# The last output of a decoder step: residual added by TensorE instead of GpSimd

## The chip, the cores and the metric

The kernel runs on one core of one Trainium2 chip. TensorE (PE) multiplies, VectorE (DVE) and ScalarE (ACT) work elementwise and read TensorE's result banks, GpSimd (POOL) works elementwise on on-chip memory alone, and SyncE (SP) issues transfers. The metric is the device time of one execution in microseconds (us); a median over several runs is given.

## The reference, cut to what matters

One inference step of a decoder layer over 520 tokens (512 of a prompt, 8 samples), width 1024. It has a SwiGLU feed-forward, a token mixer and a second SwiGLU, each between two normalizations and added to the residual:

```python
def rmsnorm(x, g):
    y = xf * lax.rsqrt(jnp.mean(xf * xf, axis=-1, keepdims=True) + EPS) * g
def swiglu(x, w_gate, w_up, w_down):
    return (jax.nn.silu(x @ w_gate) * (x @ w_up)) @ w_down
...
x = x + 0.5 * rmsnorm(swiglu(rmsnorm(x, ffn1_pre_g), ffn1_w_gate, ffn1_w_up, ffn1_w_down), ffn1_post_g)
x = x + rmsnorm(m, mix_post_g)          # m: the token mixer
x = x + 0.5 * rmsnorm(swiglu(rmsnorm(x, ffn2_pre_g), ffn2_w_gate, ffn2_w_up, ffn2_w_down), ffn2_post_g)
```

The change concerns the last line's outer part alone: the normalization of the second feed-forward's output, the addition to x, and the store of the layer's output.

## The kernel before, in words

Everything is kept transposed: the 1024 channels are 8 tiles of 128 partitions (`KD` = 8), the tokens lie along the free axis in two halves of 260 (`HC`, `HALVES`). Products are made to f32 accuracy from operands that are split into a high and a low part, three matmuls each (`passes`, L408 to L410).

The order of instructions on every engine is the order in which the Python code issues them. A product calls `tick` as it goes on, and at each tick the waiting tasks (generators that were given to `spawn`) run up to their next `yield n`, which asks for n ticks of pause. When no products are left, `finish` ticks until all tasks are done, so what stands behind the last product is issued task by task without a pause.

`down` makes the feed-forward's last product, y = W h, tile by tile; the last tile (d = 7) is made for half 0 and then for half 1 (`staged`). For each tile and half, `evac` squares the result bank on ScalarE, adds the square to `acc[hf]` on VectorE (`square_sum`, L516 and L517) and writes y = bank times gain on VectorE (L664). With the last tile of a half it spawns `post`. In `post`, `rstd` sums `acc` over the partitions with TensorE (`sums`, L471: three pieces of 87 tokens against a column of ones), VectorE makes the mean `ms` (L463), GpSimd the power -1/2 `rs` (L465), and TensorE spreads it to all partitions into the bank `rb` (`spread`, L477: three f32 products with the identity). `gnext` is None for the last output alone. Then ScalarE copies `rb` to `u` (L574), and for each of the 8 tiles t = y * rb is made (L580), x = x + t (L584) and stored by SP (L585). GpSimd makes t for the tiles 1 and 4 and the additions for 1, 4 and 6, since it cannot read `rb` it reads `u`; VectorE makes the rest. `x` holds its tiles in pairs (`x_tiles`, 128 x 2 x 260; `x_of` gives one of a pair). `self.ident` is the 128 x 128 identity in f32 (the tile `cst`). There are 8 result banks. `slot` gives on-chip tiles out of a ring.

Of the kernel before, what the change touches and what calls it, by code (L numbers as in the profile page):

```python
# [9 lines left out]
AF = mybir.ActivationFunctionType  # L10
ALU = mybir.AluOpType
# [4 lines left out]
P = 128  # L16
D = 1024
KD = D // P
# [11 lines left out]
HC = TOK // 2  # L30
HALVES = ((0, HC), (HC, HC))
PIECES, PW = 3, -(-HC // 3)
# [138 lines left out]
class Kernel:  # L171
# [371 lines left out]
    def inverse_rms(self, acc, r, plus):  # L543
# [17 lines left out]
            r[hf] = out[:, c0 : c0 + n]  # L561
        self.hold_sums = False

    def post(self, y, acc, hf, gnext, xs, r, plus, plus_next):

        nc = self.nc
        c0, n = HALVES[hf]
        cs = slice(c0, c0 + n)
        self.hold = self.hold_sums = gnext is not None
        yield 1 if gnext is None else 2  # L570
        r2 = yield from self.rstd(acc, 1.0 / D, 2 if gnext is None else 3, plus and plus[0:PW, hf * PIECES : (hf + 1) * PIECES])
        if gnext is None:
            r2s = self.work("u", n)
            nc.scalar.copy(r2s, r2)  # L574
            ts = []
            for i in range(KD + 1):
                if i < KD:
                    alone = i in (1, 4)
                    ts.append(self.slot("t", (P, n)))
                    (nc.gpsimd if alone else nc.vector).tensor_tensor(ts[i], y[i][:, cs], r2s if alone else r2, ALU.mult)  # L580
                if i:
                    k = i - 1
                    xk = self.x_of(k, hf)
                    (nc.gpsimd if k in (1, 4, 6) else nc.vector).tensor_tensor(xk, xk, ts[k], ALU.add)  # L584
                    nc.sync.dma_start(out=self.a["yT"][:, hf, k], in_=xk)  # L585
                yield 1
            return
        if not hf:
            self.rooted = False
            self.leads = 0  # L590
            self.spawn(self.pre_rms(xs, r, plus_next))
        lag = 2
        for k in range(KD + lag):
            if k < KD:
                t = self.work("t", n)
                nc.vector.tensor_tensor(t, y[k][:, cs], r2, ALU.mult)
                xk = self.x_of(k, hf)
                nc.gpsimd.tensor_tensor(xk, xk, t, ALU.add)
            if k >= lag:
                xs[hf].append(self.split_x(k - lag, hf, gnext))  # L600
            if not hf and k == 1:
                self.prefetch(True, 1)
            yield 1
        if not hf:
            self.prefetch(True, 2)
# [44 lines left out]
    def down(self, xin, pieces, gpost, gnext, held, plus=None, plus_next=None, x_from=None, seven=None):  # L650

        nc = self.nc
        y = []
        acc = [self.work(f"acc{hf}", HC) for hf in range(2)]
        xs, r = [[], []], [None, None]
        begun = set()

        def evac(d, hf, ps):
            while len(y) <= d:
                y.append(self.slot("y"))  # L660
            c0, n = HALVES[hf]
            self.square_sum(acc[hf], ps, hf, hf not in begun, nc.vector)
            begun.add(hf)
            nc.vector.tensor_scalar(y[d][:, c0 : c0 + n], ps, gpost[:, d : d + 1], None, ALU.mult)  # L664
            if d == KD - 1:
                self.spawn(self.post(y, acc[hf], hf, gnext, xs, r, plus, plus_next))

        def job():
            ws, k = [], 0
            for cnt in pieces:  # L670
                ws.append((self.next_unit(), range(k, k + cnt)))
                k += cnt
            return ws

        def load_x():
            self.x = self.x_tiles()
            for hf in range(2):
                for k in range(0, KD, 2):
                    nc.sync.dma_start(out=self.x[hf][k // 2], in_=x_from[:, hf, k : k + 2])

        for d in range(0 if seven is None else KD, KD - held):
            if d == 2 and x_from is not None:
                load_x()
            ps = self.product(job(), xin, "dn")
            for hf in range(2):
                evac(d, hf, ps[hf])
        if seven:

            rest, first8, D = seven
            xin = [rest[hf] + [None] * KD for hf in range(2)]  # L690
            xin = [Both(rest[hf], first8[hf]) for hf in range(2)]
            pieces = (7, 7, 8)
            ps = self.product(job(), xin, "dn")
            for hf in range(2):
                evac(0, hf, ps[hf])
            for d in range(1, KD - 1, 2):
                self.down_pair(rest, D, lambda z, hf, c: evac(d + z, hf, c), load_x if d == KD - 3 else None)
        self.staged([job] * held, sum(pieces), xin, "dn", lambda j, hf, ps: evac(KD - held + j, hf, ps), False)
        return xs, r
# [1194 lines left out]
```

## Time and profile before

| | |
|---|---|
| median of 3 runs | 1206.64 us (1204.07 to 1208.16) |
| the profiled execution | 1205.19 us |
| its span, first to last instruction | 1203.4 us |
| TensorE matmuls busy | 1173.8 us, 98% of the span |
| VectorE, ScalarE, GpSimd busy | 915.9, 601.7, 280.8 us |
| last down product's end | 1187.5 us |
| last elementwise instruction's end (VectorE) | 1197.1 us |
| mean granted TensorE clock | 0.991 |

Rows of a chain or timeline read: start in us, duration in us, engine, tile and line; in a timeline the bracket behind it says how long the engine had been idle and which instruction released it. Rows of groups read: line, engine, operation, output<-input, shapes, count, busy us, mean ns of one. L1878 is the program's end, where every engine waits for its own work (a DRAIN) and for the others (EVENT_SEMAPHORE); POOLq and the like are the engines' sequencers.

### The profile page before, as it was taken

The page shows a single profiled execution, that of the slowest core. Times are in us where ns is not written, and L with a number is a line of the kernel's source. Part 1 is how long each engine was busy: PE and PEld are TensorE (multiplying, and loading weights), DVE is VectorE, ACT ScalarE, POOL GpSimd, SP SyncE. Part 2 cuts the span into 40 slices and gives each one's busy share as a digit, 9 for nine tenths or more (in the row PEclk, how much of TensorE's full clock was granted, in tenths as well). Part 3 has the DMA queues.
Part 4 walks back from the last instruction along what each step waited for, and adds up shares of the span by engine and source line. Part 5 has one row for each costly group of instructions (what it writes and reads, how often), then busy time and mean ns, then how long its engine had stood idle before and what let it go on. Part 6 is the DMA issues. An engine that isn't in the chain of part 4 may idle for free. (4 is left out here: it accounts for less than half of the span.)

```text
span 1203.4 us, 25466 instructions
## 1 busy us (share of the span) xinstructions
PE 1173.8 (98%) x9805; PEld 1161.0 (96%) x9805; DVE 915.9 (76%) x1952; ACT 601.7 (50%) x1387; POOL 280.8 (23%) x502
## 2 busy tenths in 40 slices
PE   8999999999999999999999999999999999999995
PEld 8999999999999999999999999998999999999994
DVE  8988888777557788888677777757888888867554
ACT  6655666544335466313354774335565666553330
POOL 4211111000005148755541100504211111000003
PEclk8999999999999999999999999999999999999998
DMA  6787777133352433322466753242687777322352
GB/s 195 214 202 181 185 189 180 37 115 96 98 173 60 144 124 103 106 81 76 110 200 214 232 179 124 88 159 71 180 235 199 176 189 183 81 80 82 98 170 71
DMA packets 79754, 170.90 MB, mean 142 GB/s; under 512 B 17104, under 2 KB 20080, under 8 KB 79632
## 3 DMA queue, kind: packets, MB, share of 16 engines
q1 hardware_dynamic: 67344, 144.98, 37.9%
q0 software_dynamic: 12288, 24.29, 11.4%
q8 instruction: 77, 1.26, 0.4%
q14 instruction: 45, 0.37, 0.1%
HBM read 157.37 MB, written 11.86 MB: 141 GB/s over the span
## 5 line engine op out<-in xcount | busy, mean ns | idle before, releaser
L408 PE MATMUL p<-xhl,whi 128*128 128x260 f32 x784 | 230.9, 294 | 0.0
L409 PE MATMUL p<-xhl,whi 128*128 128x260 f32 x784 | 221.8, 283 | 1.4 <-DVE xhl L506 1.4
L410 PE MATMUL p<-xhl,wlo 128*128 128x260 f32 x784 | 221.2, 282 | 1.7 <-DVE wlo L351 1.7
L351 DVE TENSOR_TENSOR wlo<-raw,whi 128x1024 fp32r<-128x1024 f32 (+2 forms) x121 | 142.2, 1181 | 52.5 <-ACT whi L350 50.8
L408 PE MATMUL sv<-th,w 128*128 128x260 f32 x592 | 167.5, 283 | 0.5 <-ACT q L833 0.5
L409 PE MATMUL sv<-tl,w 128*128 128x260 f32 x592 | 167.5, 283 | 0.0
L410 PE MATMUL sv<-th,w 128*128 128x260 f32 x592 | 167.0, 282 | 0.0
L409 PEld LDWEIGHTS p<-xhl,whi 128*128 128x128 f32 x784 | 148.0, 189 | 2.0 <-DVE xhl L506 1.8
L410 PEld LDWEIGHTS p<-xhl,wlo 128*128 128x128 f32 x784 | 147.6, 188 | 2.2 <-DVE wlo L351 2.2
L408 PEld LDWEIGHTS p<-xhl,whi 128*128 128x128 f32 x784 | 147.8, 188 | 0.7
L350 ACT CAST whi<-raw 128x1024 fp32r<-128x1024 f32 (+2 forms) x121 | 116.3, 971 | 32.8 <-DMA raw<-dn_in 16.4
L307 POOL DMA_DIRECT2D s<-gu_in x74 | 65.1, 970 | 283.5 <-DMA s<-gu_in 169.1
L369 DVE TENSOR_TENSOR w<-s,w 128x512 fp32r<-128x512 f32 x148 | 101.5, 688 | 38.0 <-ACT w L368 36.7
L410 PE MATMUL dn<-hh,wlo 128*128 128x260 f32 x448 | 126.6, 283 | 1.2 <-DVE wlo L351 1.2
L408 PE MATMUL dn<-hh,whi 128*128 128x260 f32 x448 | 127.1, 284 | 0.0
L409 PE MATMUL dn<-hl,whi 128*128 128x260 f32 x448 | 126.6, 283 | 0.0
L410 PE MATMUL sv<-xhl,w 128*128 128x260 f32 x444 | 125.5, 283 | 0.0
L408 PE MATMUL sv<-xhl,w 128*128 128x260 f32 x444 | 125.4, 282 | 0.0
L409 PE MATMUL sv<-xhl,w 128*128 128x260 f32 x444 | 125.3, 282 | 0.0
L408 PEld LDWEIGHTS sv<-th,w 128*128 128x128 f32 x592 | 111.4, 188 | 0.8 <-ACT q L833 0.7
L410 PEld LDWEIGHTS sv<-th,w 128*128 128x128 f32 x592 | 111.7, 189 | 0.0
L409 PEld LDWEIGHTS sv<-tl,w 128*128 128x128 f32 x592 | 111.5, 188 | 0.0
(397 smaller groups left out, 3265.5 us busy)
## 6 DMA issues: line engine op xcount, KB each, us to landing
raw<-gu_in SPq DMA_DIRECT2D x50, 512.0 KB, 4.7
raw<-win_in SPq DMA_DIRECT2D x49, 512.0 KB, 3.6
s<-gu_in SPq DMA_DIRECT2D x74, 256.0 KB, 5.4
s<-gu_in POOLq DMA_DIRECT2D x74, 256.0 KB, 5.2
raw<-dn_in SPq DMA_DIRECT2D x32, 448.0 KB, 3.4
a<-gu_in SPq DMA_DIRECT2D x37, 256.0 KB, 5.7
x<-x SPq DMA_DIRECT2D x32, 260.0 KB, 5.2
raw<-dn_in SPq DMA_DIRECT2D x16, 512.0 KB, 3.7
```

The costliest lines, as they stand in the source:

```text
L307: self.nc.gpsimd.dma_start(out=out, in_=term, accum_op=ALU.add)
L350: self.nc.scalar.copy(hi[:, ks], t[:, ks])
L351: self.nc.vector.tensor_tensor(lo[:, ks], t[:, ks], hi[:, ks].bitcast(F32), ALU.subtract)
L369: nc.vector.tensor_tensor(w[:, 1], t[i], w[:, 0].bitcast(F32), ALU.subtract)
L408: mm(ps, hi[:, k, :], xh, start=first, stop=False, skip_group_check=more)
L409: mm(ps, hi[:, k, :], xl, start=False, stop=False, skip_group_check=more)
L410: mm(ps, lo[:, k, :], xh, start=False, stop=last, skip_group_check=more)
```

## The change

The last output gets a function of its own, `post_last`; `post` keeps the two others. Five things differ.

- y is written in pairs of tiles (`yp`, 128 x 2 x 260), apart for each half, and t is made for a pair at once (128 x 520), `rb` being read twice by a broadcast. The stores of half 0 and of half 1's last pair are for pairs.
- In half 1 the last tile's square isn't added to `acc`. TensorE sums `acc` (seven squares) and the last square `sq` apart; two `ms` follow one another on VectorE, the second taking the first as its addend.
- ScalarE's copy `u` is gone, and GpSimd's ten elementwise instructions. GpSimd makes the two powers.
- In half 1, tiles 0 to 5 are added by TensorE: the identity times x into a bank `xo` (three of these stand ahead of the spread, three behind it), then the identity times t onto it. ScalarE copies the bank into x, and SP stores each tile.
- In half 0, and for half 1's last pair, VectorE adds t to x in pairs.

```diff
+    def post_last(self, pairs, acc, sq, hf, plus):
...
+        yield 1
+        ps = self.bank("ss")
+        plus = plus[0:PW, hf * PIECES : (hf + 1) * PIECES]
+        self.sums(ps, acc, PIECES)
+        if sq is not None:
+            m = self.small("ms", [P, PIECES])
+            nc.vector.scalar_tensor_tensor(out=m[0:PW], in0=ps[0:PW, 0:PIECES], scalar=1.0 / D, in1=plus, op0=ALU.mult, op1=ALU.add)
+            plus = m[0:PW]
+            ps = self.bank("ss")
+            self.sums(ps, sq, PIECES)
+        _, r = self.root(ps, PIECES, 1.0 / D, plus)
+        banks = []
+
+        def begin(upto):
+            while len(banks) < upto:
+                banks.append(self.dbank("xo", HC))
+                mm(banks[-1], self.ident, self.x_of(len(banks) - 1, hf), start=True, stop=False, skip_group_check=True)
+
+        if hf:
+            begin(3)
+        else:
+            yield 2
+        rb = self.spread(r).unsqueeze(1).to_broadcast([P, 2, HC])
+        if hf:
+            begin(KD - 2)
+        for i in range(half):
+            x = self.x[hf][i]
+            t = self.slot("t", (P, 2, HC))
+            tt(t, pairs[hf][i], rb, ALU.mult)
+            if not hf:
+                yield 1
+            if hf and i < half - 1:
+                for z in range(2):
+                    k = 2 * i + z
+                    mm(banks[k], self.ident, t[:, z], start=False, stop=True, skip_group_check=True)
+                    nc.scalar.copy(x[:, z], banks[k])
+                    nc.sync.dma_start(out=out[:, hf, k], in_=x[:, z])
+                continue
+            tt(x, x, t, ALU.add)
+            nc.sync.dma_start(out=out[:, hf, 2 * i : 2 * i + 2], in_=x)
+            if not hf:
+                yield 1
...
@@ evac @@
+            else:
+                while len(pairs[hf]) <= d // 2:
+                    pairs[hf].append(self.slot("yp", (P, 2, HC)))
+                out = pairs[hf][d // 2][:, d % 2]
+            sq = None
+            if gnext is None and hf and d == KD - 1:
+                sq = self.work("s", n)
+                nc.scalar.activation(sq, ps, AF.Square)
+            else:
+                self.square_sum(acc[hf], ps, hf, hf not in begun, nc.vector)
             begun.add(hf)
-            nc.vector.tensor_scalar(y[d][:, c0 : c0 + n], ps, gpost[:, d : d + 1], None, ALU.mult)
-            if d == KD - 1:
+            nc.vector.tensor_scalar(out, ps, gpost[:, d : d + 1], None, ALU.mult)
+            if d == KD - 1 and gnext is None:
+                self.spawn(self.post_last(pairs, acc[hf], sq, hf, plus))
+            elif d == KD - 1:
                 self.spawn(self.post(y, acc[hf], hf, gnext, xs, r, plus, plus_next))
```

GpSimd's queue at the end of the program, as one piece of the difference. `rs` is the power; the rows below the first are those of half 0, the second power and half 1.

```order
 L465 TENSOR_TENSOR rs_16353<-ms_16351,mhalf 87x3
-L580 TENSOR_TENSOR t_16381<-y_15439,u_16371 128x260
-L584 TENSOR_TENSOR x_16168<-x_16168,t_16381 128x260
-L580 TENSOR_TENSOR t_16411<-y_15844,u_16371 128x260
-L584 TENSOR_TENSOR x_16170<-x_16170,t_16411 128x260
-L584 TENSOR_TENSOR x_16171<-x_16171,t_16431 128x260
-L465 TENSOR_TENSOR rs_16455<-ms_16453,mhalf 87x3
-L580 TENSOR_TENSOR t_16467<-y_15439,u_16463 128x260
-L584 TENSOR_TENSOR x_16172<-x_16172,t_16467 128x260
-L580 TENSOR_TENSOR t_16479<-y_15844,u_16463 128x260
-L584 TENSOR_TENSOR x_16174<-x_16174,t_16479 128x260
```

One more addition, for tile 7, follows before; now the second power is the queue's last work.

TensorE's queue before, from the last three of the down product's matmuls to the end:

```order
L408 MATMUL dn_2776_16334<-hp_2609_15109,whi_2771_16258 128x260
L409 MATMUL dn_2776_16334<-hp_2609_15109,whi_2771_16258 128x260
L410 MATMUL dn_2776_16334<-hp_2609_15109,wlo_2772_16259 128x260
L471 MATMUL ss_2791_16449<-ones_93,acc1_2579_14927 87x1 x3
L477 MATMUL rb_2794_16459<-cst_122,rs_2793_16455 128x87 x3
```

And now, behind the same three matmuls (`ss` are the sums, `xo` the banks of the addition, `cst` is the identity):

```order
L471 MATMUL ss_2786_16432<-ones_93,acc1_2579_14927 87x1 x3
L471 MATMUL ss_2788_16438<-ones_93,s_2785_16429 87x1 x3
L586 MATMUL xo_2791_16446<-x_2750_16172,cst_122 128x260
L586 MATMUL xo_2792_16448<-x_2750_16172,cst_122 128x260
L586 MATMUL xo_2793_16450<-x_2751_16173,cst_122 128x260
L477 MATMUL rb_2794_16452<-cst_122,rs_2790_16444 128x87 x3
L586 MATMUL xo_2795_16456<-x_2751_16173,cst_122 128x260
L586 MATMUL xo_2796_16458<-x_2752_16174,cst_122 128x260
L586 MATMUL xo_2797_16460<-x_2752_16174,cst_122 128x260
L604 MATMUL xo_2791_16446<-t_2798_16462,cst_122 128x260
L604 MATMUL xo_2792_16448<-t_2798_16462,cst_122 128x260
```

Four more of L604 follow. Three products moved ahead of the spread, and nine stand behind it where there was nothing.

VectorE's queue now, from the last tile's y to the end; before, sixteen instructions of 128x260 stood here (acc, y, one t and one x of half 0, `ms`, then eleven of half 1):

```order
L710 TENSOR_SCALAR yp_2766_16232<-dn_2776_16334,gh_124 128x260
L576 SCALAR_TENSOR_TENSOR ms_2787_16436<-ss_2786_16432,plus2_13_128 87x3
L463 SCALAR_TENSOR_TENSOR ms_2789_16442<-ss_2788_16438,ms_2787_16436 87x3
L598 TENSOR_TENSOR t_2798_16462<-yp_2617_15153,rb_2794_16452 128x520
L598 TENSOR_TENSOR t_2799_16470<-yp_2672_15518,rb_2794_16452 128x520
L598 TENSOR_TENSOR t_2800_16478<-yp_2715_15867,rb_2794_16452 128x520
L598 TENSOR_TENSOR t_2801_16486<-yp_2766_16232,rb_2794_16452 128x520
L608 TENSOR_TENSOR x_2753_16175<-x_2753_16175,t_2801_16486 128x520
```

The addition to `acc` is gone from here, the mean has become two instructions, and one of half 1's four pairs is still added here.

More of the change, by code (lines that the diff above doesn't have):

```diff
@@ L562, in inverse_rms @@
         self.hold_sums = False
+    def post_last(self, pairs, acc, sq, hf, plus):
+        nc = self.nc
+        tt, mm = nc.vector.tensor_tensor, nc.tensor.matmul
+        half = KD // 2
+        out = self.a["yT"]
+        yield 1
[38 more added lines that the diff above has]
+                yield 1
     def post(self, y, acc, hf, gnext, xs, r, plus, plus_next):
@@ L568, in post @@
         cs = slice(c0, c0 + n)
[L569 to L587, printed above, removed]
+        self.hold = self.hold_sums = True
+        yield 2
+        r2 = yield from self.rstd(acc, 1.0 / D, 3, plus and plus[0:PW, hf * PIECES : (hf + 1) * PIECES])
         if not hf:
@@ L656, in down @@
         begun = set()
+        pairs = [[], []]
         def evac(d, hf, ps):
-            while len(y) <= d:
-                y.append(self.slot("y"))
             c0, n = HALVES[hf]
-            self.square_sum(acc[hf], ps, hf, hf not in begun, nc.vector)
+            if gnext is not None:
+                while len(y) <= d:
+                    y.append(self.slot("y"))
+                out = y[d][:, c0 : c0 + n]
+            else:
[8 more added lines that the diff above has]
+                self.square_sum(acc[hf], ps, hf, hf not in begun, nc.vector)
             begun.add(hf)
-            nc.vector.tensor_scalar(y[d][:, c0 : c0 + n], ps, gpost[:, d : d + 1], None, ALU.mult)
-            if d == KD - 1:
+            nc.vector.tensor_scalar(out, ps, gpost[:, d : d + 1], None, ALU.mult)
+            if d == KD - 1 and gnext is None:
+                self.spawn(self.post_last(pairs, acc[hf], sq, hf, plus))
+            elif d == KD - 1:
                 self.spawn(self.post(y, acc[hf], hf, gnext, xs, r, plus, plus_next))
```

## Prediction

> **What bounds the kernel now.** I read the page's head first, then the chain of waits over the last 16 us, because the diff touches only the last output.
>
> ```profile
> span 1203.4 us, 25466 instructions
> PE 1173.8 (98%) x9805; PEld 1161.0 (96%) x9805; DVE 915.9 (76%) x1952; ACT 601.7 (50%) x1387; POOL 280.8 (23%) x502
> ```
>
> TensorE is busy for 98% of the span, and nothing of the change lies under its long run of products. What can move is the tail behind the last product. Its chain, rows of half 1:
>
> ```profile
> 1187.53 0.40 ACT s L516
> 1187.95 0.43 DVE acc L517
> 1188.38 0.40 DVE y L664
> 1188.78 0.33 DVE t L580
> 1189.11 0.15 DVE ms L463
> ...
> 1189.33 1.00 POOL rs L465
> ...
> 1190.38 0.92 PE rb L477 x6
> ...
> 1191.32 0.38 ACT u L574
> ...
> 1191.72 0.44 DVE t L580
> ...
> 1192.71 0.74 DVE t L580 x2
> ...
> 1196.61 0.51 DVE x L584
> ```
>
> The last square waits for nothing but the last product (1187.51). Then come the addition to the sum of squares, the mean `ms`, GpSimd's power `rs`, its spread over the partitions `rb`, ScalarE's copy `u`, and sixteen elementwise instructions until 1197.12. But the chain ends at 1197.12 and the span at 1203.4. What fills the 6.3 us between is in the instructions of the program's end, L1878 (first four rows: the whole trace, with shortest/median/longest duration in ns and first and last start; then the stretch 1198 to 1200; then 1202.5 to 1202.75):
>
> ```profile
> L1878 POOLq DRAIN  x3: 51/93/6696, 1195.9 to 1203.1; - x3
> L1878 PEldq DRAIN  x2: 13/475/937, 1190.4 to 1203.0; - x2
> L1878 ACTq DRAIN  x2: 14/210/406, 1191.3 to 1202.9; - x2
> L1878 DVEq DRAIN  x2: 19/283/547, 1196.6 to 1202.9; - x2
> ...
> L1878 SPq EVENT_SEMAPHORE  x8: 28/28/28, 1199.1 to 1199.5; - x8
> L1878 SPq DRAIN  x2: 7/7/7, 1199.6 to 1199.6; - x2
> ...
> L1878 POOLq EVENT_SEMAPHORE  x1: 17/17/17, 1202.7 to 1202.7; - x1
> ```
>
> The last store has landed at 1199.1, when SP's eight end waits begin, and SP is through at 1199.6. TensorE, ScalarE and VectorE ended their drains with their last work (1196.6 + 0.55 = 1197.15 for VectorE). GpSimd's drain began at 1195.9 and took 6.70 us: until 1202.6. The end follows 0.8 us later. So **the kernel ends with GpSimd's drain**, 3.0 us after SP was ready. GpSimd's last work, and the stores that SP issued in half 1:
>
> ```profile
> 1195.98 0.85 POOL L584 TENSOR_TENSOR x<-x,t 128x260 f32<-128x260 f32 x1 [1.04 <-DVE t L580]
> 1192.81 0.92 SPq L585 DMA_DIRECT2D yT_out<-x  x2
> 1196.86 0.81 SPq L585 DMA_DIRECT2D yT_out<-x  x2
> yT_out<-x SPq DMA_DIRECT2D x8, 130.0 KB, 1.8
> ```
>
> The drain outlasts the last GpSimd instruction (end 1196.83) by 5.8 us. Two issues in a row stand 0.47 us apart (0.81 - 0.34), so the last store was issued at 1197.33 and landed 1.77 us later.
>
> **The change part by part.** *1. Last square's sums apart.* Gone from the path are acc, y and a left-over t of half 0 between square and `ms`. The prices:
>
> ```profile
> 1188.44 0.62 PE L471 MATMUL ss<-ones,acc 128*87 128x1 f32 x6 [0.94 <-DVE acc L517]
> 1188.30 0.48 DVE L664 TENSOR_SCALAR y<-dn,gh 128x260 f32<-128x260 f32 x1
> 1182.44 0.38 ACT L574 COPY u<-rb 128x260 f32<-128x260 f32 x1 [3.57 <-PE rb L477]
> L537 DVE TENSOR_TENSOR sq<-sq,sq 128x520 f32<-128x520 f32 x14 | 9.8, 699 | 0.6
> ```
>
> The first three sums (of the seven older squares) run right behind the last product, under ScalarE's square, which ends at 1187.93. The second three start at 1187.99 and end at 1188.61 (0.62); the second mean runs from 1188.65 to 1188.80, the power from 1188.87 instead of 1189.33: **-0.46**. VectorE must be free: y starts when the square ends (1187.97, 0.48), the first mean follows by 1188.5. Ahead of them in its queue stand half 0's eight instructions of 128x520, at 0.70 us each with the 0.1 us overlap of independent neighbours: from 1182.44 (rb is done; it waits no more for ScalarE) to about 1187.85. That is 0.1 us of cover; were it missing, each tenth over it would be lost.
>
> *2. Power, spread, ScalarE's copy.* The power stays 1.00, to 1189.87. TensorE's three x products stand ahead of the spread now; it is free from 1188.57 to 1189.91. For their price there is no row of 128x260 in plain f32; the nearest:
>
> ```profile
> 500.03 0.39 PE L1353 MATMUL po<-st,rp 128*128 128x128 f32 x2
> 500.26 0.39 PE L1354 MATMUL po<-rv,sT 128*128 128x128 f32 x2
> L1545 PE MATMUL pV<-pack,AT 32*32 32x32 f32 x64 | 2.3, 194 | 0.0
> L1167 PE MATMUL tr<-cst,cv 128*128 128x128 f32 x48 | 7.4, 277 | 0.0
> L408 PE MATMUL p<-xhl,whi 128*128 128x260 f32 x784 | 230.9, 294 | 0.0
> ```
>
> One f32 product is two records. With 128 columns the pair takes 0.225 us, 0.11 a record. A record grows from 194 to 277 ns between 32 and 128 columns, 0.86 ns a column; 260 columns give 260 x 0.86 = 0.22 a record, **0.44 a product**. The bounds: 0.24, if a record costs the 0.12 us at which the 128x260 records of the long products follow each other (1173.8 us / 9805), and 0.88, if the clock is halved. I take 0.44, from the f32 rows. Three are 1.32, until 1189.89: just under the power, so the spread is not late. It ends at 1190.83. The copy `u` is gone, with its two gaps: t starts at 1190.87 instead of 1191.72. **-0.39** more.
>
> *3. The elementwise part.* VectorE: four t of 0.70 (0.6 apart), then one addition of 0.70; done at about 1194.1. TensorE: the spread's issue is over at 1190.67 (0.17 before its end), three x products to 1191.99, by then the first t (1191.57) is there; six t products to 1194.63, the result 0.17 later (277 ns of a record less its 0.11), ScalarE's copy 0.38 (each hides under the next product), so SP issues the sixth store at 1195.25 and the pair's store, waiting behind it, 0.47 later at 1195.72. TensorE's nine products set this, not VectorE. Before: 1197.33. The last issue is **-1.61** early, of which steps 1 and 2 made 0.85; 0.76 is new. With 0.24 a product, SP's seven issues of 0.47 become the bound and it is another 0.45.
>
> *4. The last store is twice as long* (260 KB for 130 KB):
>
> ```profile
> 1198.20:1198.40 0.20, 0.00 (x0) 0.00 (x0) 0.00 (x0) 0.00 (x0) 0.00 (x0) 0.50 0.84 302
> 1198.60:1198.80 0.20, 0.00 (x0) 0.00 (x0) 0.00 (x0) 0.00 (x0) 0.00 (x0) 0.50 0.08 21
> ```
>
> (stretches: us, busy of PE, PEld, DVE, ACT, POOL, then clock, DMA share, GB/s). 133 KB more at 302 GB/s: **+0.44**; the bounds are 0 (the other stores of half 1 are through, the path has room) and 0.9 (half the rate, behind a backlog). Landing: 1195.72 + 1.77 + 0.44 = 1197.93, SP ready at 1198.45.
>
> *5. GpSimd only makes the power.* Its five elementwise instructions of half 1 go to VectorE and TensorE (paid in 3). Its last work ends at 1189.87, and a drain of 5.8 us behind it ends at 1195.7, 2.8 us before SP. Then SP is last and the end stands 0.8 us behind it: 1199.25. Removed: **-3.0**, the time from SP's readiness to the drain's end. Bounds: 0, if the drain ends by something else than its own work, and 3.0, which is all there is.
>
> *6. At no cost:* the pair tiles for y (same number of tiles; the first writes into the last pair wait for old products, as y's did), four stores of half 0 in place of eight, and half 0's additions on VectorE, all under the last stage's products.
>
> Sum: -0.46 - 0.39 - 0.76 + 0.44 - 3.0 = **-4.2 us**. The profiled execution took 1205.19 (span 1203.4): 1201.0 after. The median shown is 1206.64, 1.45 above it, so I forecast **1202.4**.
>
> **The rivals.** *The drain stays.* If its 6.7 us hang on the end of the other engines or on the last store (it ended 3.5 us after that landed) and not on GpSimd's own last instruction, term 5 is nothing and 1.2 us are left: 1205.4. For it: no other long drain is in this trace to show what sets it. Against: it is a bare drain without a wait, begun next to the last GpSimd instruction, and three other engines' drains ended with their own work.
>
> *TensorE cold or f32 dearer, the slower side.* The clock after the spread of before:
>
> ```profile
> 1191.00:1192.00 1.00, 0.28 (x3) 0.12 (x2) 0.28 (x1) 0.38 (x1) 0.23 (x1) 1.00 0.00 0
> 1192.00:1193.00 1.00, 0.00 (x0) 0.00 (x0) 0.96 (x3) 0.00 (x0) 0.92 (x2) 0.84 0.00 0
> 1193.00:1194.00 1.00, 0.00 (x0) 0.00 (x0) 1.00 (x3) 0.00 (x0) 1.00 (x2) 0.50 0.34 115
> ```
>
> The granted clock falls to half at about 1192.7, 1.4 us after TensorE's last work. With P a product, the last issue is at 1188.57 + 12 P + 1.85 once 3 P outlasts the power; the gain of 3.0 less 0.44 is eaten at 1199.9, so from P = 0.79 the change loses. At 0.88 the issue is at 1200.98 and the time 1.1 us longer: 1207.7. Against it: the clock was still 1.00 after 1.3 us of waiting for the power, and after the change that gap is filled with products. The Trainium skill, "TensorE: Matmul & The Clock Gate", Part 1 (the HAM clock gate), says that a free-running window of about 3.4 us in which the array is idle halves the clock. By that rule nine products without a gap would stay at full clock and the sum would stand; a window that happens to close early, as the drop 1.4 us after the spread suggests, speaks for this rival.
>
> *The products at 0.24:* 0.45 better, 1202.0; it lies in the first case's range.
>
> **How the numbers follow.** The forecast (drain hidden, products between 0.24 and about 0.5) 0.80, drain stays 0.15, TensorE cold 0.05. The bound of about 0.3%, what a measurement of this kernel can tell from no change, is 3.6 us. The three runs lie from 1204.07 to 1208.16, so a median is uncertain by over 1 us. A gain of 4.2 is over 3.6 in two of three such measurements: 0.53 from the first case, 0.02 from the second, none from the third: faster 0.55; same 0.42; slower 0.03. Range: down to 1200.0 (all bounds on the good side, -5.1, and the median's scatter of 1.5), up to 1206.0 (the drain stays and 0.6 of scatter).
>
> **What would show it.** In the profile after: the power about 1.4 us behind the last product's end instead of 1.8; no ScalarE instruction between spread and first t; GpSimd's drain still 6 to 7 us long but begun near the power and over before SP's last end wait; records of `xo` 0.22 us apart at clock 1.00; the last store issued some 8.2 us after the last product (9.8 before). Wrong would be: a drain that ends later than SP again, a clock of 0.50 before the sixth store, or VectorE late for the mean because half 0 is not done at 1187.9.

## The result, and the profile after

| | before | after |
|---|---|---|
| median | 1206.17 us (9 runs, from 1204.07) | 1202.42 us (9 runs, 1200.28 to 1203.04) |
| profiled execution, its span | 1205.19, 1203.4 | 1200.41, 1198.6 |
| last down product's end | 1187.51 | 1187.05 |
| from there to the span's end ("the tail") | 15.89 | 11.55 |

The ratio of after to before is 0.9967, 95% interval 0.9958 to 0.9977; one run of before at 1908.33 us is left out of it. The forecast was 1202.4. Of the 4.8 us between the two spans 4.34 lie in the tail; 0.46 lie ahead of the last product, where the change leaves TensorE's products as they were; in the variants of the changed kernel below, that point lies anywhere between 1186.44 and 1190.54, so this is scatter. All comparisons of single profiles below are therefore made by the tail. A span is given to 0.1 us, and a tail from one profile is no finer than that.

The chain of waits of the changed kernel, behind the last product (start, duration, engine, tile, line):

```profile
1186.91 0.14 PE dn L410
...
1187.07 0.40 ACT s L706
...
1187.51 0.62 PE ss L471 x6
1188.14 1.42 PE xo L586 x6
1189.56 0.65 PE rb L477 x6
1190.21 1.35 PE xo L586 x6
1191.56 2.64 PE xo L604 x12
...
1194.23 0.38 ACT x L605
```

Where VectorE, GpSimd and ScalarE took turns before, TensorE works from 1187.51 to 1194.2 almost without a gap. A product of 128x260 in f32 costs 1.42 / 3 = 0.47, 1.35 / 3 = 0.45 and 2.64 / 6 = 0.44 us. The other engines' rows from the timeline, with what each waited for in brackets:

```profile
1188.41 0.85 POOL L465 TENSOR_TENSOR rs<-ms,mhalf 87x3 f32<-87x3 f32 x1 [7.50 <-DVE ms L463]
1190.25 2.52 DVE L598 TENSOR_TENSOR t<-yp,rb 128x520 f32<-128x520 f32 x4 [1.92 <-PE rb L477]
1192.04 2.57 ACT L605 COPY x<-xo 128x260 f32<-128x260 f32 x6 [4.58 <-PE xo L604]
1192.44 2.79 SPq L606 DMA_DIRECT2D yT_out<-x  x6
1195.32 0.40 SPq L609 DMA_DIRECT2D yT_out<-x  x1
```

The power starts 1188.41 - 1187.05 = 1.36 us behind the last product (1.82 before). The first t starts 3.20 behind it (4.21 before), but its first pair is ready at about 1190.94, and TensorE comes to it only at 1191.56. The last store is issued 8.27 behind the last product (9.82 before). Now the program's end, whose line is L1926 here: three rows of the whole trace, then one of the stretch 1197.2 to 1198.

```profile
L1926 SPq EVENT_SEMAPHORE  x11: 17/28/28, 1195.8 to 1198.5; - x11
L1926 POOLq DRAIN  x3: 51/102/6689, 1188.4 to 1198.3; - x3
L1926 SPq DRAIN  x3: 7/7/7, 1197.8 to 1198.1; - x3
...
L1926 SPq EVENT_SEMAPHORE  x6: 17/28/28, 1197.5 to 1198.0; - x6
```

GpSimd's drain is still there and as long as ever, 6.69 us, but it begins at 1188.4 with the power and is over at 1195.1. The last store has landed at 1197.5, SP is ready at 1197.8, and the end follows 0.8 later: SP, not GpSimd, is last by 2.7 us. The stores and the clock (stretch, busy of the five engines, granted clock, DMA share, GB/s):

```profile
1193.20:1196.90 3.70, 0.99 (x5) 0.53 (x3) 0.30 (x1) 1.22 (x4) 0.00 (x0) 1.00 0.81 284
1197.60:1198.60 1.00, 0.00 (x0) 0.00 (x0) 0.00 (x0) 0.00 (x0) 0.00 (x0) 1.00 0.00 0
```

The clock stayed at 1.00 to the end, and half 1's output moved in one stretch of 3.7 us at 284 GB/s; before, the same bytes trickled out over about 5 us.

### The profile page after: what moved, and what is told of

It reads as the page before. It is cut to its first block, busy times and chain, and to the rows that moved or that the text cites. A ratio compares the mean times of both kernels' runs of the same rounds, so it can differ in the third digit from the quotient of the medians.

```text
span 1198.6 us, 25498 instructions
## 1 busy us (share of the span) xinstructions
PE 1179.1 (98%) x9835; PEld 1165.9 (97%) x9835; DVE 913.7 (76%) x1943; ACT 603.1 (50%) x1391; POOL 273.5 (23%) x492
## 3 DMA queue, kind: packets, MB, share of 16 engines
q0 software_dynamic: 12288, 24.29, 11.1%
```

## The experiments

Four questions: what sets GpSimd's drain, whether it alone makes the gain, which of the other steps lie on the path, and what sets the end now.

**1. A late GpSimd instruction.** An addition of 128x520 whose result nobody reads is put on GpSimd behind the last VectorE addition.

```diff
+            if hf:
+                z = self.slot("z", (P, 2, HC))
+                nc.gpsimd.tensor_tensor(z, x, t, ALU.add)
```

> The changed kernel with one more GpSimd instruction (128x520, into a tile that nothing reads) behind half 1's last addition on VectorE, which ended at 1193.50 in the changed kernel's profile. If the end of the program waits for GpSimd's drain, the drain begins near 1193.5 and, at its 6.69 us of both profiles, ends near 1200.2 (or near 1200.8 if it is 5.83 us behind the end of an instruction of some 1.5 us); the tail from the last product to the end grows from 11.55 to 13.9 to 14.6 us and the time from 1202.4 to 1204.8 to 1205.4. Rival: the gain came from the shorter chain and the stores alone, the drain is no cause: the tail stays 11.55 and the time 1202.4.

Measured: 1202.97 us (10 runs), ratio to the kernel before 0.9983 (0.9973 to 0.9992). The timeline's row of the added instruction, the two drains, and the head of the page (last product's end 1186.54):

```profile
span 1201.0 us, 25500 instructions
1193.15 1.28 POOL L612 TENSOR_TENSOR z<-x,t 128x520 f32<-128x520 f32 x1 [4.41 <-DVE x L608]
L1929 POOLq DRAIN  x3: 51/102/7107, 1193.1 to 1200.7; - x3
L1929 SPq DRAIN  x3: 7/7/7, 1197.2 to 1200.5; - x3
```

SP is ready at 1197.2 and waits until the drain ends at 1200.2; the tail is 14.5, 2.9 longer than without the addition, as expected. The time missed the expectation: 1202.97 for 1204.8 to 1205.4. The kernel before was faster beside it (1205.24), but that makes up only 0.9 of it. By the ratios (0.9967 and 0.9983) the addition cost 0.16%, about 1.9 us, and with the width of the two intervals anything from 0 to 4 us fits, so the weight lies on the tail. The drain has become longer (7.11 us), and ends 5.8 us behind the addition's end (1194.43).

**2. The same with a tiny instruction**, a copy of 128x1 in the same place:

```diff
+            if hf:
+                z = self.small("z", [P, 1])
+                nc.gpsimd.tensor_copy(z, x[:, 0, 0:1])
```

> As the run before, but the added GpSimd instruction copies a 128x1 column. If the drain is 6.69 us from its own start, its end is the same as with the long instruction, near 1200.2 on the changed kernel's clock, tail 13.9 us; if it is 5.83 us behind the last instruction's end, it ends a good 1 us earlier than with the long one, tail about 13.2 us. Rival without the drain: tail 11.55 us.

Measured: one run, 1205.6 us, all of it later ahead of the tail (last product's end 1190.54), so only the tail is read: 13.26.

```profile
span 1203.8 us, 25499 instructions
1197.05 0.19 POOL L612 COPY z<-x 128x1 f32<-128x1 f32 x1 [4.31 <-DVE x L608]
L1929 POOLq DRAIN  x3: 51/102/6017, 1197.0 to 1203.6; - x3
```

This drain takes 6.02 us and again ends 5.8 us behind the instruction's end (1197.24). So the drain follows GpSimd's own last instruction by a fixed 5.8 us, whatever that instruction was; its row is longer only because it begins while the instruction still runs. The rival that it hangs on the stores or the other engines has fallen: in the changed kernel the drain was over at 1195.1, before the last store was issued (1195.32).

**3. The kernel before without GpSimd in half 1.** All else of the change is left out; VectorE makes all sixteen elementwise instructions of half 1.

```diff
-            alone = i in (1, 4)
+            alone = not hf and i in (1, 4)
...
-    (nc.gpsimd if k in (1, 4, 6) else nc.vector)
+    (nc.gpsimd if not hf and k in (1, 4, 6) else nc.vector)
```

> The kernel before with one part of the change alone: GpSimd's five elementwise instructions of half 1 go to VectorE, everything else as before (no product adds, no pairs, the ScalarE copy stays). Sixteen VectorE instructions of 128x260 at 0.34 us apart end at about 1197.2, as the mixed ones did (1197.12). By the drain theory the drain is over at about 1196 and the end stands 0.8 us behind SP's 1199.6: 1200.4, tail from 15.9 to 12.9 us, time 1203.2 for 1206.2 of before (ratio 0.9975). Rival: the drain is no cause, tail 15.9 or a little longer, ratio 1.000.

Measured: 1201.85 us (10 runs), ratio 0.9975 (0.9965 to 0.9984), the ratio that was expected.

```profile
1188.08 0.99 POOL L465 TENSOR_TENSOR rs<-ms,mhalf 87x3 f32<-87x3 f32 x1 [1.31 <-DVE ms L463]
L1878 POOLq DRAIN  x3: 51/93/6832, 1188.0 to 1198.9; - x3
L1878 SPq DRAIN  x3: 7/7/7, 1198.4 to 1198.7; - x3
```

Its last square starts at 1186.28, so the last product ended at about 1186.26 and the tail is 1199.2 - 1186.26 = 12.94: 2.95 less than before. About two thirds of the tail's gain (2.95 of 4.34) are had by two edited conditions. VectorE alone is done at 1195.96, 9.70 behind the last product; with GpSimd's help it was 9.61. VectorE's own additions took up to 0.97 us beside GpSimd's and 0.42 alone. So GpSimd's help saved 0.1 us of work and cost 3.0 at the end.

**4. The last square back into `acc`**, in the changed kernel:

```diff
-            if gnext is None and hf and d == KD - 1:
+            if False:
                 sq = self.work("s", n)
```

> The changed kernel with the last square added to acc again by VectorE and the sums made once, as in the kernel before; all else stays. The tail from the last product's end to the span's end is 11.55 us in the changed kernel. Theory (step 1 is worth its 0.46 us and all of it lies on the path): the power starts about 1.8 us behind the last product instead of 1.36, and the tail is 12.0 us. Rival (the x products and the stores set the end, the power's start has room): the tail stays within 0.15 of 11.55.

Measured (one run, 1203.31; its chain):

```profile
span 1201.5 us, 25483 instructions
1189.36 0.14 PE dn L410
...
1189.52 0.40 ACT s L516
1189.94 0.44 DVE acc L517
1190.43 0.62 PE ss L471 x6
1191.05 1.42 PE xo L586 x6
```

The tail is 1201.5 - 1189.50 = 12.0. Everything behind the sums has the changed kernel's durations, only later: step 1 is worth its 0.45 in full.

**5. ScalarE's copy `u` back between spread and t**, in both halves:

```diff
-        rb = self.spread(r).unsqueeze(1).to_broadcast([P, 2, HC])
+        rb = self.spread(r)
+        u = self.work("u", HC)
+        nc.scalar.copy(u, rb)
+        rb = rb.unsqueeze(1).to_broadcast([P, 2, HC])
```

> The changed kernel with ScalarE's copy u put back between the spread and the first t of each half: t waits for it, and begins about 0.4 us later. By the prediction's step 2 the copy costs its 0.39 us on the path: tail 11.9 us in place of 11.55. Rival, read from the changed kernel's trace (the first t is ready at 1190.94, TensorE is busy with the x products until 1191.56): TensorE's nine products set the end, a t that is ready at 1191.34 is still in time, and the tail stays 11.5 to 11.6.

Measured: one run, 1202.42, last product's end 1188.71, span 1200.6: tail 11.89, as the prediction's step 2 has it. But the profile shows another way to it. From the timeline:

```profile
1188.81 0.70 DVE L611 TENSOR_TENSOR x<-x,t 128x520 f32<-128x520 f32 x1
1190.32 0.84 POOL L465 TENSOR_TENSOR rs<-ms,mhalf 87x3 f32<-87x3 f32 x1 [7.74 <-DVE ms L463]
1192.15 0.38 ACT L594 COPY u<-rb 128x260 f32<-128x260 f32 x1 [3.03 <-PE rb L477]
1193.31 2.90 PE L607 MATMUL xo<-t,cst 128*128 128x260 f32 x12
```

The copy of half 0 made half 0's additions later: the last ends 0.80 behind the last product, in the changed kernel 0.38. That held up VectorE's y and the mean, and the power starts at 1.61 instead of 1.36. So 0.25 of the 0.34 came from half 0. This number alone would have confirmed a wrong reason.

**6. The copy in half 1 alone** tells the two apart:

```diff
+        if hf:
+            u = self.work("u", HC)
+            nc.scalar.copy(u, rb)
```

> The changed kernel with ScalarE's copy u put back in half 1 alone. With the copy in both halves the tail was 11.89 in place of 11.55, but there half 0's additions had also become 0.4 us later, and the power started 1.61 instead of 1.36 us behind the last product. Here half 0 is untouched, so the power starts at 1.36 again, the first t about 3.6 behind the last product (3.20 without the copy). Theory (the copy lies beside TensorE's x products, which end 4.51 behind the last product, when the first t is ready at about 4.3): tail 11.5 to 11.65. Rival (the copy is on the path with its 0.39): 11.9.

Measured: one run, 1200.4, span 1198.6; its chain:

```profile
1186.81 0.14 PE dn L410
...
1190.10 1.35 PE xo L586 x6
1191.46 2.75 PE xo L608 x12
```

The power is at 1.36 again, TensorE turns to the t products 4.51 behind the last product as without the copy, and they take 2.75 instead of 2.64. The tail is 1198.6 - 1186.95 = 11.65. The copy costs 0.10 here, not 0.39. That holds with TensorE's additions in place. Where VectorE makes them (experiment 3 with the copy, experiment 7 without), the first t starts 1.34 and 0.94 us behind the spread's start, so there the copy delays VectorE by 0.40.

**7. No additions on TensorE**: VectorE adds all four pairs of half 1 (`begin` and its products left out).

```diff
-            if hf and i < half - 1:
+            if False:
```

> The changed kernel without TensorE's additions: in half 1 VectorE adds all four pairs, and all four are stored as pairs. VectorE then has eight instructions of 128x520, 0.70 us each with 0.1 overlap of neighbours that do not wait for each other: from 3.1 us behind the last product (no x products ahead of t) to about 8.2 to 8.6, so the last store is issued at 8.2 to 8.6 where it was 8.27. Theory (VectorE on whole pairs is nearly as fast; the gain of step 3 comes from pairs and the missing GpSimd steps): tail 11.5 to 11.9. Rival (the 0.76 us of step 3 hang on TensorE's additions): tail 12.3.

Measured: one run, 1200.26, span 1198.5. From the timeline, the last addition, and SP's drains:

```profile
1189.63 0.70 DVE L594 TENSOR_TENSOR t<-yp,rb 128x520 f32<-128x520 f32 x1 [1.92 <-PE rb L477]
...
1194.39 0.70 DVE L604 TENSOR_TENSOR x<-x,t 128x520 f32<-128x520 f32 x1
...
L1922 SPq DRAIN  x3: 7/7/7, 1197.7 to 1198.0; - x3
```

The last square starts at 1186.46, the last product ended at 1186.44. VectorE is done 8.65 behind it, just past the upper end of what I expected, and the tail is 12.06, between the theory (11.5 to 11.9) and the rival (12.3). TensorE's twelve products, with ScalarE's copies, are worth about 0.5 us against three more additions on VectorE: something, but the smaller part of the gain.

**8. Four tiles on TensorE, two pairs on VectorE**, a better balance by the issue times:

```diff
-            begin(KD - 2)
+            begin(KD - 4)
...
-            if hf and i < half - 1:
+            if hf and i < half - 2:
```

> The changed kernel with four tiles added by TensorE and two pairs by VectorE in half 1. If the last store's issue sets the end (TensorE's nine products behind the spread and seven issues in a row), the last issue comes at 1194.3 in place of 1195.32 and the tail falls from 11.55 to 10.5 us, time 1201.4. Rival: the stores are bound by their transfer (1.07 MB at the 284 GB/s of the changed kernel): the last byte comes only as much earlier as the first store does, 0.5 us: tail 11.05. Second rival: nothing, since the end hangs elsewhere: 11.55.

Measured: 1201.61 us (5 runs), ratio 0.9968 (0.9955 to 0.998), the changed kernel has 0.9967. Last product's end 1187.01, span 1198.1, tail 11.1.

```profile
1193.99 0.88 SPq L609 DMA_DIRECT2D yT_out<-x  x2
L1926 SPq DRAIN  x3: 7/7/7, 1197.2 to 1197.5; - x3
```

The last issue came 0.8 us earlier (two in 0.88, the second at about 1194.47, so 7.46 behind the last product), the tail shrank by 0.45. That is the first rival's number (11.05) and not the theory's (10.5). Its reason does not carry: the two pairs, issued 0.47 apart, landed 2.2 to 2.4 us behind their issue instead of 2.15, and the 284 GB/s are looked at under the next experiment.

**9. The last pair's store on ScalarE's queue** instead of behind six issues on SP:

```diff
-            nc.sync.dma_start(out=out[:, hf, 2 * i : 2 * i + 2], in_=x)
+            (nc.scalar if hf else nc.sync).dma_start(out=out[:, hf, 2 * i : 2 * i + 2], in_=x)
```

> The changed kernel with half 1's last pair's store issued by ScalarE, behind its six copies, in place of SP, where it waits behind six other issues: the issue moves from 8.27 to about 7.6 us behind the last product. If the last issue sets the end: tail 10.9 us in place of 11.55. Rival (the 910 KB of half 1's stores move at about 284 GB/s, the transfer engines set the end): tail 11.3 to 11.55.

Measured: one run, 1202.81, last product's end 1189.48, span 1201.0: tail 11.52. The issue, and the stretch in which half 1's output moved; then the stores of half 1 with the median time from issue to landing in us, first in the changed kernel, then here (of its six single tiles the slowest took 2.1 and 2.6):

```profile
1196.71 0.40 ACTq L609 DMA_DIRECT2D yT_out<-x  x1
1195.60:1199.20 3.60, 1.02 (x5) 0.55 (x3) 0.32 (x1) 1.24 (x4) 0.00 (x0) 0.99 0.85 296
...
yT_out<-x SPq DMA_DIRECT2D x6, 130.0 KB, 1.8
yT_out<-x SPq DMA_DIRECT2D x1, 260.0 KB, 2.1
...
yT_out<-x SPq DMA_DIRECT2D x6, 130.0 KB, 2.0
yT_out<-x ACTq DMA_DIRECT2D x1, 260.0 KB, 2.4
```

The last pair is issued 7.23 behind the last product, 1.04 us earlier than in the changed kernel, and the tail is the same within 0.03. But the last issue is now the sixth single tile's on SP, at 1197.26, 7.78 behind the last product and just where it stood in the changed kernel. Both stores landed later than stores with more room between them: the pair after 2.4 us, the slowest single tile after 2.6. The reading is that the two shared the transfer, which moved 357 GB/s in the stretch from 1198 to 1199, and that it held up the end here.

In the changed kernel that is not so. Its single tiles landed 1.7 to 2.1 us behind their issue, those of the kernel before 1.7 to 1.9, so hardly anything waits. The 284 GB/s match the pace of SP's issues: six stand (2.79 - 0.40) / 5 = 0.48 us apart, and 133 KB every 0.48 us are 277 GB/s. (Half 1 has eight tiles, 1.06 MB; the 910 KB that I wrote are one tile short.)

**10. and 11. All of half 1 stored in pairs**, once with six tiles on TensorE (its edit is shown), once with four (with the edits of experiment 8 as well).

```diff
-                    nc.sync.dma_start(out=out[:, hf, k], in_=x[:, z])
+                nc.sync.dma_start(out=out[:, hf, 2 * i : 2 * i + 2], in_=x)
                 continue
```

> The changed kernel, with the six tiles that TensorE adds stored as three pairs, behind every second of ScalarE's copies, so SP issues four stores in half 1 in place of seven. The last copy ends 7.56 behind the last product in the changed kernel, and SP then has no backlog: the last issue moves from 8.27 to about 7.6. In the traces stores of single tiles moved at about 280 GB/s, stores of pairs at 380 to 409. Theory (the rate and the issues of single tiles set the end): tail 10.8 to 11.0. Rival (half 1's bytes as such set the end, whatever their pieces): 11.4 to 11.55.

> The changed kernel with four tiles added by TensorE, two pairs by VectorE, and all of half 1 stored as pairs. VectorE's last addition ends 7.2 behind the last product, SP has no backlog, so the last issue stands at about 7.2 and the last pair lands 1.8 to 2 later. Theory (single-tile stores were the limit with four tiles, tail 11.1): tail 10.4 to 10.6, some 1 us better than the changed kernel, ratio to the kernel before 0.996. Rival (nothing more is to be had behind the last issue): tail 11.1, ratio 0.9967.

Measured with six: one run, 1201.37, last product's end 1187.92, span 1199.6, tail 11.68. With four: 1200.76 us (6 runs), ratio 0.9962 (0.995 to 0.9974), last product's end 1188.06, span 1199.3, tail 11.24. SP's rows of the first, then of the second with two stretches of its transfer:

```profile
1193.74 2.09 SPq L606 DMA_DIRECT2D yT_out<-x  x3
1195.92 0.41 SPq L609 DMA_DIRECT2D yT_out<-x  x1
...
1193.59 1.21 SPq L606 DMA_DIRECT2D yT_out<-x  x2
1194.89 0.90 SPq L609 DMA_DIRECT2D yT_out<-x  x2
1195.00:1196.00 1.00, 0.00 (x0) 0.00 (x0) 0.24 (x1) 0.00 (x0) 0.00 (x0) 1.00 0.84 312
1196.00:1197.00 1.00, 0.00 (x0) 0.00 (x0) 0.00 (x0) 0.00 (x0) 0.00 (x0) 1.00 1.01 385
```

Both theories fell short: pairs do move faster (up to 385 GB/s), but their first store is issued later (5.82 and 5.53 behind the last product, 5.39 with single tiles) since it waits for two tiles, and with six tiles the last pair stood behind the third on SP, which I had overlooked. The tails lie on the rivals' side, with six tiles even above the rival's 11.4 to 11.55.

What sets the end now can be read across the runs. In the changed kernel and in experiments 4, 5 and 6, which leave its stores alone, the tail ends 3.27 to 3.28 us behind the last issue, wherever that lies (8.27 to 8.73). There the last issue sets the end. In experiments 8 to 11 the last stores are issued earlier or closer together, and the end stands 3.6 to 3.9 us behind the last issue: part of each gain goes into a longer landing. These are single profiles. None of the variants is shown to beat the changed kernel: the intervals of 0.9962, 0.9967 and 0.9968 overlap almost wholly.

## Why the prediction was right, step by step

The sum was -4.2 us for the tail; it measured -4.34. The difference is about what a term makes that the sum did not have: SP is ready 0.3 us behind the last landing (1197.5 to 1197.8), before it was 0.5.

- *Step 5, the drain (-3.0): right, and shown.* Experiments 1 and 2 show that the drain hangs on GpSimd's last instruction; experiment 3, which has nothing but this step, gave -2.95. The rival "the drain stays" is out.
- *Step 1, the last square (-0.46): right, and shown.* The power stands 0.46 closer to the last product, and experiment 4 gives 0.45 back. The cover of 0.1 us on VectorE was at least as thin as said: half 0 ended 0.38 behind the last product, and in experiment 5, where it ended at 0.80, the power slipped by 0.25.
- *Step 2, the copy `u` (-0.39): the size was wrong in this kernel.* Experiment 6 measured 0.10; the 0.39 would hold where VectorE makes the additions. The prediction's own step 3 had the reason in it: the first t at 1191.57, TensorE free for it at 1191.99. A t that is early by 0.42 cannot make the end 0.39 earlier.
- *Step 3 (-0.76): too small by what step 2 had too much.* The two together were to be -1.15, with step 1 -1.61 for the last issue; it measured -1.55. The split was mis-stated, the sum was not. Of the gain about 0.5 hangs on the additions on TensorE (experiment 7). The absence of GpSimd's steps gave nothing (experiment 3); what the pairs alone gave was not taken apart. The step also named TensorE's products as what sets the last issue. The sixth copy ended at 1194.61, but SP came to its store only at 1194.83: SP's 0.48 an issue was slower than the 0.44 a product, by 0.2 in sum.
- *Its price of a product, 0.44 from the f32 rows of 32 and 128 columns: right* (0.44 to 0.47). The three products ahead of the spread ran to 1189.56, 0.30 behind the power's end (1189.26), where the kernel before had 0.05. So the spread was about 0.25 late, which the prediction had at nothing: 0.15 because the power took 0.85 and not 1.00, 0.10 because the three took 1.42 and not 1.32. The spread itself took 0.65 and not 0.92, which made up for it.
- *Step 4 (+0.44): right in size, and its reason fits.* The last store landed 2.15 us behind its issue, +0.38. In experiment 7 the four pairs are issued 1.34 us apart and each lands 2.0 behind its issue; the single tiles of experiment 3 take 1.7 to 1.8. So about 0.3 is the store's own double length, and some 0.1 is left for the stores ahead of it. The backlog, the prediction's upper bound, shows only where stores stand closer together (experiments 8 to 11).
- *TensorE cold: did not happen.* The clock was 1.00 through all nine products. By the Trainium skill, "TensorE: Matmul & The Clock Gate", Part 1, an idle window of about 3.4 us has to pass before the clock halves. The trace of the changed kernel agrees, with TensorE busy to 1194.2. The trace of experiment 3 does not: its clock fell at 1190.63, 0.6 us behind TensorE's last work, and in the 3.4 us ahead of the fall TensorE had worked for 1.5. So the fall does not need an idle stretch of that length, and what would cause it stays open; shown is that the nine products ran at 1.00.

The median's agreement to 0.02 us is luck: the median of the runs scatters by about a microsecond. The kernel before moved too, from the 1206.64 that the forecast started from to 1206.17, so the medians differ by 3.75 and not by 4.2. The ratio says 0.33%, with an interval from 0.23% to 0.42%; whether the gain lies past the 0.3% that was called faster is therefore not shown. The tail, term by term, is the firmer ground.

## What to carry to other kernels

Look at the program's end, not only at the last work: an engine's own drain can outlast everything, and then the cheapest edit is to let that engine finish early, even if another has to do its share. Here the other engine lost only 0.1 us by it. When a step is credited with its duration, check in the same reckoning that what it releases is waited for; the slack of one step is not gained twice. An experiment that confirms a number should also be read for how it came about, since here a copy put back in both halves gave the right number for the wrong reason.

## What had not been expected of the hardware

- GpSimd's last long drain ends 5.8 us behind its last instruction in all kernels here, with rows of 6.70, 6.69, 7.11, 6.02 and 6.83 us.
- The clock's fall after TensorE's last work is not at a fixed distance: 0.6 us in experiment 3, 1.4 us in the kernel before, over 4.4 us in the changed one (still 1.00 at the span's end). The Trainium skill, "TensorE: Matmul & The Clock Gate", Part 1, describes a window that runs freely, which fits the spread. That TensorE be idle in the whole window does not fit the 0.6 us, and no run here shows the window itself.
- A store's length shows little in its landing as long as stores have room: 1.7 to 1.8 us for 130 KB, 2.0 for 260 KB. Single tiles moved at about 284 GB/s, the pace of SP's issues (one every 0.48 us), pairs at up to 385. With stores issued closer together the landings grew to 2.3 to 2.6 us, and no order of the stores tried here moved the tail by more than half a microsecond.
